# Addresses of stationary and moving operands in a hybrid decoder layer on one core

## Chip, cores and metric

One core of a Trainium2 chip runs the whole layer. The metric is the device time of one execution in microseconds (us); less is better. Spans, starts and durations of single instructions come from one profiled execution.

## The reference

`x` is 1 x 512 x 1024 in float32, and all products are wanted at float32 accuracy. Cut to what matters:

```python
h = rmsnorm(x, norm_mix_g)
q, k, v, xr, gr, g_attn, g_rnn = jnp.split(h @ w_in, offs, axis=-1)      # each 512 x 1024
attn_out = diff_attention(q, k, v, ...)        # 8 heads, two softmaxes a head, causal
rnn_out  = rg_lru_branch(xr, gr, ...)          # conv, gates, linear recurrence
merged = sigmoid(g_attn) * (attn_out @ w_pa) + sigmoid(g_rnn) * (rnn_out @ w_pr)
x = x + merged @ w_out
up = square(relu(rmsnorm(x) @ w_up))           # 512 x 4096
x = x + up @ w_down
```

## The kernel before

Every operand of a product is split into two float32r tiles, a high part and the rest, and a product is three matmuls: high x high, high x rest, rest x high (`mm3`, lines 124 to 127). The first operand named is the stationary one, loaded into TensorE 128 columns at a time; the second is the moving one, streamed past it with 256 or 512 columns. The stationary tile of the next matmul is loaded while the present one streams.

Weights come in units of 128 x 1024 (4 blocks of 128 rows, 256 columns). A load on SP's queue brings a unit into a raw buffer; ScalarE copies it to `whi`, VectorE writes the rest to `wlo` (`Weights.cast`, line 98; in the last stages `cast_hi` and `cast_lo`, lines 914 to 942). Four pairs of slots in pool `wp` hold cast units, and in the last stages every fifth unit (`own`, line 920) uses a pair in pool `fin` instead. A unit takes part in 24 matmuls. TensorE's instructions run in the order in which the program emits them; the other engines have an order of their own, kept by hand (`InOrder`).

The stages in order of time:

- The first gate blocks (lines 265 to 338): `hu` moving (512 columns), weights stationary. `two(k)` multiplies two blocks at once; the third block goes through `cols_proj` (line 137) with `hu` too. Then `hT`, the normalised input, is written over the pool `hp`.
- q, k, v (`qkv_pair`, `tok_proj`, line 220): here `hT` is stationary and the weights move, 256 columns. They fill the pauses of `attention` (line 492), whose logits multiply `qkT` tiles with each other, whose transposes have `pe` or `qn` stationary and `ident` moving (lines 459 and 541), and whose value product (`av`, line 547) has `v` stationary and `pt` moving, 256 columns.
- The remaining gates and the recurrent branch (`rnn_chunk`): `hT` moving, 512 columns. `y_attn` (line 742) multiplies `w_pa` with the attention's output `aT` between them.
- `y_rnn` (line 750) with `R` moving, then `merged` (line 834) with `mT` moving, all 512 columns.
- The MLP, from line 1054: three up pairs and then alternately down and up. An up step has `h2T` moving, 512 columns. A down step (line 1093, seven products in place of eight by sums of blocks) has `us` moving, 256 columns, in four stages of 336 matmuls (d = 0 to 3); stage d reads `forms[2d]` and `forms[2d + 1]`. `forms[n]` stands in `hp` if n % 3 is 0, else in `fin` as `us1` or `us2` (`up_out`, line 979).

In the built program the tiles begin, in bytes of a partition modulo 256, at: weight slots of `wp` 64; `hT`, `mT` and the `us` of `hp` 64; `hu`, `h2T`, `R`, `pt`, `v`, `pe`, `qn`, `ident`, the own slots and the `us` of `fin` 128; `qkT` and `aT` 224. All blocks within a tile lie a multiple of 512 bytes apart, so that the tiles' beginnings alone set the difference of two operands modulo 256.

GpSimd issues few DMAs: two small ones a head, and 16 in the down stages that add one raw block to another (lines 935 and 940). Their descriptors stand in a space at the beginning of each partition.

Of the kernel before, what the change touches and what calls it, by code (L numbers as in the profile page):

```python
# [11 lines left out]
F32 = mybir.dt.float32  # L12
F32R = mybir.dt.float32r
# [6 lines left out]
P = 128  # L20
# [3 lines left out]
KT = DM // P  # L24
# [13 lines left out]
def tile_block(ctx: ExitStack, tc: tile.TileContext, x, w_in, w_rga, w_rgx, w_pa, w_pr, w_o,  # L38
               w_up, w_dn, rel_bias, smalls, lamv, onehot, out):
    nc = tc.nc  # L40
# [3 lines left out]
    wp = ctx.enter_context(tc.tile_pool(name="wp", bufs=3))  # L44
# [33 lines left out]

    slots = [4]

    class Weights:
        def __init__(self, ahead, raws):
            self.reqs, self.raw, self.units = [], [], []
            self.pos, self.done, self.ahead, self.raws = 0, 0, ahead, raws

        def cols(self, w, c0, k0=0, n=KT):
            for k0 in range(k0, k0 + n, 4):
                self.reqs.append((w[k0 // 4, c0 // 256], 4))
            return self

        def fetch(self):
# [3 lines left out]
                nc.sync.dma_start(raw, src.rearrange("p (k c) -> p k c", k=a))  # L95
                self.raw.append(raw)

        def cast(self, pool=None):
            assert pool or slots[0] > 0
            slots[0] -= 0 if pool else 1  # L100
            self.fetch()
            n = len(self.units)
            raw, a = self.raw[n], self.reqs[n][1]
            hi, lo = ((pool or wp).tile([P, a, 1024 // a], F32R, tag=t, name=t, bufs=2 if pool else 4) for t in ("whi", "wlo"))
            A.copy(hi, raw)
            V.tensor_tensor(out=lo, in0=raw, in1=hi.bitcast(F32), op=ALU.subtract)
            self.raw[n] = None
            self.units.append((hi, lo))
            self.fetch()
# [121 lines left out]
    wa.cols(w_in, OGA + 512)  # L231
    for j in range(4):
        for o in (OQ, OK_, OV):
            wa.cols(w_in, o + 256 * j)
    wa.cols(w_in, OGA + 768)
    for j in range(4):
        wa.cols(w_in, OGR + 256 * j)
    for j in range(4):
        wa.cols(w_pa, 256 * j)
    wb = Weights(1, 1)  # L240
    for j in range(4):
        wb.cols(w_in, OX + 256 * j).cols(w_in, OG + 256 * j)
    for j in range(4):
        wb.cols(w_pr, 256 * j)
    for j in range(4):
        wb.cols(w_o, 256 * j)
    R, aT, mT = [None] * KT, [None] * NH, [None] * KT
# [17 lines left out]
    with tc.tile_pool(name="p1", bufs=1) as p1:  # L265
        on = p1.tile([P, P], F32, name="on")
        G.memset(on, 1.0)
        zero = p1.tile([P, 256], F32R, name="zero")
        V.memset(zero.bitcast(F32), 0.0)
        pw = psum("acc")  # L270
        for n in range(16):
            T.matmul(pw[:, :256], zero[:, :P], zero, start=True, stop=True)
        ssq = p1.tile([P, S], F32, name="ssq")
        xT = p1.tile([P, KT, S], F32, name="xT")
        hu = [p1.tile([P, KT, S], F32R, name=f"hu{z}", tag=f"hu{z}") for z in range(2)]
        raws = [[(wp if u else p1).tile([P, 4, 256], F32, name="wraw", tag="wraw", bufs=2) for u in range(2)] for z in range(2)]
        pieces = ((0, 1), (1, 2), (2, 4), (4, 6), (6, 8))
        for k0, k1 in pieces:
            nc.sync.dma_start(xT[:, k0:k1, :], x[k0 * P:k1 * P, :].rearrange("(k p) s -> p k s", p=P))
            if k0 == 0:  # L280
                nc.sync.dma_start(smt, smalls)
            for z in range(2):
                c0 = 256 * (k0 % 4)
                nc.sync.dma_start(raws[z][k0 // 4][:, k0 % 4:(k1 - 1) % 4 + 1, :],
                                  w_in[k0 // 4, OGA // 256 + z][:, c0:c0 + 256 * (k1 - k0)].rearrange("p (k c) -> p k c", c=256))
        wa.fetch()
        ws = [[[wp.tile([P, 4, 256], F32R, tag=t, name=t, bufs=4) for t in ("whi", "wlo")] for u in range(2)] for z in range(2)]
        ps = [[psum("at"), psum("at")] for z in range(2)]
        for k0, k1 in pieces:
            u, kk = k0 // 4, slice(k0 % 4, (k1 - 1) % 4 + 1)  # L290
            for k in range(k0, k1):
                split(hu[0][:, k, :], hu[1][:, k, :], xT[:, k, :], smt[:, C_G1 + k:C_G1 + k + 1])
                if k == k0:
                    for z in range(2):
                        split(ws[z][u][0][:, kk, :], ws[z][u][1][:, kk, :], raws[z][u][:, kk, :])
            for k in range(k0, k1):
                sq = ssq if k == 0 else p1.tile([P, S], F32, tag="sq", name="sq", bufs=2)
                A.activation(sq, xT[:, k, :], AF.Square)
                if k:
                    V.tensor_tensor(out=ssq, in0=ssq, in1=sq, op=ALU.add)  # L300

        def two(k):
            for z in range(2):
                for c in range(2):
                    w = ws[z][k // 4]
                    cs = slice(c * P, (c + 1) * P)
                    mm3(ps[z][c], (w[0][:, k % 4, cs], w[1][:, k % 4, cs]), (hu[0][:, k, :], hu[1][:, k, :]), k == 0, k == KT - 1)

        for k in range(6):
            two(k)  # L310
        slots[0] = 2
        wa.cast()
        pr = psum("at")
        for t in range(NT):
            T.matmul(pr[:, t:t + 1], ssq[:, t * P:(t + 1) * P], ones, start=True, stop=True)
        rs = sm.tile([P, NT], F32, tag="rs4", name="rs4")
        rstd_of(rs, pr[:, :NT], DM, NT)
        dg = p1.tile([P, S], F32, name="dg", tag="sq", bufs=2)
        for t in range(NT):
            A.activation(dg[:, t * P:(t + 1) * P], ident, AF.Copy, scale=rs[:, t:t + 1])  # L320
        two(6)
        wa.cast()
        rb = p1.tile([P, S], F32, name="rb")
        gu = cols_proj(wa, lambda k: (hu[0][:, k, :], hu[1][:, k, :]), lambda ps: gate_out(tga, 2, ps, rb))
        pb = psum("acc")
        T.matmul(pb, on, dg, start=True, stop=True)
        V.tensor_copy(rb, pb)
        two(7)
        slots[0] += 2
        for k in range(KT + 1):  # L330
            if k < KT:
                V.tensor_tensor(out=xT[:, k, :], in0=xT[:, k, :], in1=rb, op=ALU.mult)
            if k > 0:
                split(hT[0][:, k - 1, :], hT[1][:, k - 1, :], xT[:, k - 1, :], smt[:, C_G1 + k - 1:C_G1 + k])
                next(gu)
        wa.pump()
        for z in range(2):
            gate_out(tga, z, ps[z], rb)
# [19 lines left out]
    for half in range(2):  # L358
        PT.append([wk.tile([P, 2 + 2 * half, 256], F32R, name=f"pt{half}{z}", tag=f"pt{half}{z}") for z in range(2)])
        for z in range(2):  # L360
            G.memset(PT[half][z][:, 1 + 2 * half, 0:P].bitcast(F32), 0.0)

    def work(name):
        return wk.tile([P, S], F32, tag="pe", name=name, bufs=5)
# [549 lines left out]
    def cast_hi():  # L914
        n = len(units)
        plus(n)
        slots[0] -= 1
        kind, a, p = ops[n]
        src = raw[kind, a, p if kind == "up" else uses[p][0]]
        own = n % 5 == 4  # L920
        hi, lo = ((fin if own else wp).tile([P, 4, 256], F32R, tag=t, name=t, bufs=1 if own else 4) for t in ("whi", "wlo"))
        A.copy(hi, src)
        units.append((hi, lo))
        half.append((hi, lo, src, ops[n]))
# [54 lines left out]
    def up_out(a, ps):  # L979
        n = a // 2  # L980
        if a % 2 == 0:
            forms[n] = (hp if n % 3 == 0 else fin).tile([P, 2, 7, 2, 256], F32R, tag=("hT", "us1", "us2")[n % 3], name="us")
        d = forms[n][:, :, :, a % 2, :]
        q = fin.tile([P, 2, 2, 256], F32, tag="q", name="q")
        fs = fin.tile([P, 4, 256], F32, tag="fs", name="fs")
        w = 0.0 if a == 15 else 1.0
        for c in range(2):
            A.activation(q[:, c, ::-1, :], two(ps[c]), AF.Relu)
            A.activation(q[:, c], q[:, c], AF.Square)
        a11, a21, a22, a12 = q[:, 0, 1], q[:, 0, 0], q[:, 1, 0], q[:, 1, 1]  # L990

        def sums():
            for m, (x, y, op) in enumerate(((a21, a22, ALU.subtract), (fs[:, 0], a11, ALU.subtract), (a11, a21, ALU.subtract), (a12, fs[:, 1], ALU.add))):
                V.tensor_tensor(out=fs[:, m], in0=x, in1=y, op=op)

        def first_hi():
            hi_part(d[:, :, 0], a11)
            hi_part(d[:, :, 1:3], q[:, 1])

        def first_lo():  # L1000
            lo_part(d[:, :, 0], a11)
            lo_part(d[:, :, 1:3], q[:, 1])

        later(w * 1.0, first_hi)
        if w == 0:
            later(0.0, first_lo)
        later(w * 2.5, sums)
        later(w * 3.5, lambda: hi_part(d[:, :, 3:7], fs))
        if w:
            later(3.6, first_lo)  # L1010
        later(w * 5.0, lambda: lo_part(d[:, :, 3:7], fs))
# [129 lines left out]
```

## Time and profile before

| | |
|---|---|
| median of 3 runs | 881.33 us (881.31 to 881.35) |
| the profiled execution | 880.92 us |
| its span, first to last instruction | 879.2 us |
| TensorE: matmuls, busy | 5232, 871.2 us (99%) |
| TensorE: weight loads, busy | 5232, 762.6 us (87%) |
| VectorE, ScalarE, GpSimd busy | 602.2, 429.0, 64.4 us |
| DMA moved | 99.28 MB, 113 GB/s |

Matmuls overlap in the profile: the next one starts while the one before is still draining, so the mean length of one says little on how often one starts. Weight loads are a row of their own (PEld) and run beside the matmuls. In the table of windows a row gives the stretch, its length, the time TensorE was busy in it, in brackets the matmuls that lie in it or reach into it, the granted clock (1.00 is all of it), the DMA engines' busy share and GB/s.

### The profile page before, as it was taken

What the parts mean: (1) busy time and instruction counts of PE and PEld (TensorE: products, weight loads), DVE (VectorE), ACT (ScalarE), POOL (GpSimd) and SP (SyncE); (2) the same over time, 40 slices, a digit from 0 to 9 for tenths busy, and PEclk for the clock granted to TensorE, in tenths of its full rate; (3) what the DMA queues carried; (4) which work ended last, traced back from release to release, by engine and by line L of the source; (5) the groups of instructions that cost most, each with busy time, mean ns of one, the idle gap of its engine ahead of it and who ended that gap; (6) DMA issues with size and microseconds to landing.
All of it is one profiled execution on the core that took longest, in us unless ns stands there. A gap on an engine that the chain in (4) does not pass through costs nothing.

```text
span 879.2 us, 13193 instructions
## 1 busy us (share of the span) xinstructions
PE 871.2 (99%) x5232; PEld 762.6 (87%) x5232; DVE 602.2 (68%) x1040; ACT 429.0 (49%) x683; POOL 64.4 (7%) x72
## 2 busy tenths in 40 slices
PE   9999999999999999999999999999999999999997
PEld 7799999999888887888878888889988998899897
DVE  6765688887866346877876656767746775667586
ACT  7444355554555336577643235556335444544441
POOL 0030222113000000000000000000000000000000
PEclk9999999999999999999999999999999999999999
DMA  5347222131321342322213633223642364256353
GB/s 200 135 142 222 93 73 77 52 94 62 98 70 39 113 137 95 110 85 88 80 55 125 223 125 114 102 86 82 170 166 72 110 173 134 64 137 194 78 146 95
DMA packets 34238, 99.28 MB, mean 113 GB/s; under 512 B 3952, under 2 KB 8760, under 8 KB 34176
## 3 DMA queue, kind: packets, MB, share of 16 engines
q1 hardware_dynamic: 30976, 87.93, 30.3%
q0 software_dynamic: 3200, 10.50, 6.3%
q8 instruction: 41, 0.67, 0.3%
q14 instruction: 21, 0.17, 0.1%
HBM read 87.89 MB, written 4.76 MB: 105 GB/s over the span
## 4 chain that ended last, share of the span: by engine, by line
PE 88%; ACT 4%; DMA 3%; DVE 3%; issue 1%; SPq 0%; POOL 0%; ACTq 0%; DVEq 0%; POOLq 0%
PE acc L125 21%; PE acc L126 21%; PE acc L127 20%; PE acc L1093 17%; PE at L507 3%; DMA wraw<-in_w_in_dram 2%; ACT whi L66 1%; DVE wlo L66 1%; PE at L541 1%; PE at L126 1%; PE at L127 1%; PE at L125 1%; PE at L459 1%; PE at L572 1%; DMA xT<-in_x_dram 1%
## 5 line engine op out<-in xcount | busy, mean ns | idle before, releaser
L1093 PE MATMUL acc<-us,whi 128*128 128x256 f32 x896 | 158.9, 281 | 0.5 <-DVE x L66 0.5
L66 DVE TENSOR_TENSOR wlo<-wraw,whi 128x1024 fp32r<-128x1024 f32 (+2 forms) x86 | 96.9, 1148 | 67.9 <-ACT whi L66 67.6
L66 ACT CAST whi<-raw 128x1024 fp32r<-128x1024 f32 x88 | 90.5, 1048 | 104.2 <-DVE raw L66 39.4
L1093 PEld LDWEIGHTS acc<-us,whi 128*128 128x128 f32 x896 | 137.7, 189 | 1.2 <-DVE x L66 0.7
L1093 PE MATMUL acc<-us,wlo 128*128 128x256 f32 x448 | 125.4, 280 | 0.0
L66 DVE TENSOR_TENSOR wlo<-raw,whi 128x1024 fp32r<-128x1024 f32 x88 | 106.8, 1220 | 17.1 <-ACT whi L66 17.0
L125 PE MATMUL acc<-whi,hT 128*128 128x256 f32 x384 | 111.4, 290 | 0.0
L127 PE MATMUL acc<-whi,hT 128*128 128x256 f32 x384 | 108.9, 284 | 0.0
L126 PE MATMUL acc<-wlo,hT 128*128 128x256 f32 x384 | 108.9, 284 | 0.0
L66 ACT CAST whi<-wraw 128x1024 fp32r<-128x1024 f32 (+2 forms) x86 | 82.5, 982 | 50.0 <-DMA wraw<-in_w_in_dram 33.6
L126 PE MATMUL acc<-h2T,whi 128*128 128x512 f32 x256 | 100.5, 392 | 0.0
L125 PE MATMUL acc<-h2T,whi 128*128 128x512 f32 x256 | 100.1, 391 | 0.0
L127 PE MATMUL acc<-h2T,wlo 128*128 128x512 f32 x256 | 100.0, 390 | 0.0
L1093 PEld LDWEIGHTS acc<-us,wlo 128*128 128x128 f32 x448 | 84.2, 188 | 0.0
L125 PE MATMUL acc<-hT,whi 128*128 128x512 f32 x208 | 82.2, 395 | 0.0
L127 PE MATMUL acc<-hT,wlo 128*128 128x512 f32 x208 | 81.5, 392 | 0.0
L126 PE MATMUL acc<-hT,whi 128*128 128x512 f32 x208 | 81.5, 392 | 0.0
L125 PEld LDWEIGHTS acc<-whi,hT 128*128 128x128 f32 x384 | 73.2, 191 | 4.3 <-issue 3.0
L127 PEld LDWEIGHTS acc<-whi,hT 128*128 128x128 f32 x384 | 73.2, 191 | 0.8 <-issue 0.4
L126 PEld LDWEIGHTS acc<-wlo,hT 128*128 128x128 f32 x384 | 73.3, 191 | 0.7 <-issue 0.5
L66 ACT ACTIVATE pe<-pe,nm 128x128 f32<-128x128 f32 (+3 forms) x64 | 35.5, 556 | 65.4 <-DVE nm L66 65.4
L66 DVE TENSOR_TENSOR x<-acc,x 128x512 f32<-128x512 f32 x48 | 33.0, 688 | 40.9 <-PE acc L1093 31.5
(194 smaller groups left out, 1609.9 us busy)
## 6 DMA issues: line engine op xcount, KB each, us to landing
wraw<-in_w_in_dram SPq DMA_DIRECT2D x52, 512.0 KB, 3.5
raw<-in_w_up_dram SPq DMA_DIRECT2D x32, 512.0 KB, 4.4
raw<-in_w_dn_dram SPq DMA_DIRECT2D x32, 512.0 KB, 3.4
raw<-raw POOLq DMA_DIRECT2D x16, 512.0 KB, 4.5
wraw<-in_w_pa_dram SPq DMA_DIRECT2D x8, 512.0 KB, 4.3
wraw<-in_w_pr_dram SPq DMA_DIRECT2D x8, 512.0 KB, 3.4
wraw<-in_w_o_dram SPq DMA_DIRECT2D x8, 512.0 KB, 4.4
trep<-tdram SPq DMA_DIRECT2D x8, 320.0 KB, 4.9
```

Source lines behind the costliest of these rows:

```text
L66: ins = f(*a, **k)
L125: T.matmul(o, l[0], r[0], start=first, stop=False)
L126: T.matmul(o, l[0], r[1], start=False, stop=False)
L127: T.matmul(o, l[1], r[0], start=False, stop=last)
L459: T.transpose(out=ps[:, t * P:(t + 1) * P], in_=qn[t // 2][:, c0:c0 + P], identity=ident)
L507: T.matmul(lg[c][:, :N], qT[r, x0, i * P:(i + 1) * P], kT[r, y0, :N], start=a == 0, stop=a == 2)
L541: T.transpose(out=tp[:, b * P:(b + 1) * P], in_=st[s][:, b * P:(b + 1) * P], identity=ident)
L572: T.matmul(ps[:, t:t + 1], sq[:, t * P:(t + 1) * P], ones, start=True, stop=True)
L1093: T.matmul(b[:, 256 * u:256 * u + 256], l[:, i, P * u:P * u + P], act[:, r, f, i % 2], start=p in ("M1", "M2", "M5") and k == z == u == e ...
```

## The change

Only places in memory change; every instruction, its operands and its order stay.

- A slot for `whi` or `wlo` becomes 256 bytes longer, and a unit stands in it shifted by 0, 64 or 160 bytes (`weight_pair`). The shift is 64 for the first two gate blocks, for q, k, v, for `w_pr`, and for up and down in the shared slots; 160 for `w_pa`; 0 elsewhere, in the own slots too.
- The `us` tiles in `fin` become 256 bytes longer and are used from byte 192 on.
- A tile `apart` of 64 bytes stands ahead of `pe`, `qn`, `v` and the attention's output tiles.
- The space for descriptors of GpSimd's DMAs shrinks from 16384 (the default) to 8192 bytes of each partition, which makes the room.
- `cols` and `cast` lose parameters that nobody used.

By these sizes (8192, 4352 and 28928 bytes are multiples of 256) the difference of the moving operand's address and that of the stationary one, modulo 256, becomes:

| product (stationary, moving), columns | before | after |
|---|---|---|
| first two gate blocks (weights, `hu`), 512 | 64 | 0 |
| third gate block (weights, `hu`), 512 | 64 | 64 |
| q, k, v (`hT`, weights), 256 | 0 | 64 |
| value product (`v`, `pt`), 256 | 0 | 192 |
| transposes (`pe` or `qn`, `ident`), 128 | 0 | 192 |
| gates and recurrent inputs (weights, `hT`), 512 | 0 | 0 |
| `y_attn` (weights, `aT`), 512 | 160 | 0 |
| `y_rnn` (weights, `R`), 512 | 64 | 0 |
| output (weights, `mT`), 512 | 0 | 0 |
| up (weights, `h2T`), 512: shared, own slot | 64, 0 | 0, 0 |
| down (weights, `us` of `hp`), 256: shared, own slot | 0, 192 | 192, 192 |
| down (weights, `us` of `fin`), 256: shared, own slot | 64, 0 | 192, 192 |

```diff
+    def weight_pair(shift, own=None):
+        ts = [(own or wp).tile([P, 1024 + 64], F32R, tag=t, name=t, bufs=1 if own else 4) for t in ("whi", "wlo")]
+        return [t[:, shift // 4:shift // 4 + 1024].rearrange("p (k c) -> p k c", k=4) for t in ts]
...
-        def cols(self, w, c0, k0=0, n=KT):
-            for k0 in range(k0, k0 + n, 4):
+        def cols(self, w, c0, shift=0):
+            for k0 in range(0, KT, 4):
                 self.reqs.append((w[k0 // 4, c0 // 256], 4))
+                self.shift.append(shift)
...
-            hi, lo = ((pool or wp).tile([P, a, 1024 // a], F32R, tag=t, name=t, bufs=2 if pool else 4) for t in ("whi", "wlo"))
+            hi, lo = weight_pair(self.shift[n])
...
         for o in (OQ, OK_, OV):
-            wa.cols(w_in, o + 256 * j)
+            wa.cols(w_in, o + 256 * j, 64)
...
-        wa.cols(w_pa, 256 * j)
+        wa.cols(w_pa, 256 * j, 160)
...
-        wb.cols(w_pr, 256 * j)
+        wb.cols(w_pr, 256 * j, 64)
...
-        ws = [[[wp.tile([P, 4, 256], F32R, tag=t, name=t, bufs=4) for t in ("whi", "wlo")] for u in range(2)] for z in range(2)]
+        ws = [[weight_pair(64) for u in range(2)] for z in range(2)]
...
+    wk.tile([P, 16], F32, name="apart")
...
         own = n % 5 == 4
-        hi, lo = ((fin if own else wp).tile([P, 4, 256], F32R, tag=t, name=t, bufs=1 if own else 4) for t in ("whi", "wlo"))
+        hi, lo = weight_pair(0 if own else 64, fin if own else None)
...
-            forms[n] = (hp if n % 3 == 0 else fin).tile([P, 2, 7, 2, 256], F32R, tag=("hT", "us1", "us2")[n % 3], name="us")
+            t = hp.tile([P, 7168], F32R, tag="hT", name="us") if n % 3 == 0 else fin.tile([P, 7168 + 64], F32R, tag=f"us{n % 3}", name="us")
+            t = t if n % 3 == 0 else t[:, 48:48 + 7168]
+            forms[n] = t.rearrange("p (r f h s) -> p r f h s", r=2, f=7, h=2)
...
-    nc = _bacc.Bacc("TRN2", target_bir_lowering=False, num_devices=1)
+    nc = _bacc.Bacc("TRN2", target_bir_lowering=False, num_devices=1, dynamic_dma_scratch_size=8192)
```

## Rows read from the trace of the kernel before

**Rows 1.** The page's head: the span, and busy time, share and instructions of each engine.
```profile
span 879.2 us, 13193 instructions
PE 871.2 (99%) x5232; PEld 762.6 (87%) x5232; DVE 602.2 (68%) x1040; ACT 429.0 (49%) x683; POOL 64.4 (7%) x72
```

**Rows 2.** The list of waits of TensorE's matmuls, the first and the last of six: total us, times, longest.
```profile
PE acc L272 <- DVE zero L66: 1.2, 1, 1.2
...
PE at L125 <- ACT tt L66: 0.2, 1, 0.2
```

**Rows 3.** Windows of TensorE over stretches of 512 columns, in this order: `hT` (83 matmuls), `mT` (192), `h2T` with an own slot (24), `R` (120), `h2T` with shared slots (96), `aT` (20).
```profile
292.15:310.97 18.82, 18.82 (x85) 1.00 0.39 112
495.02:538.59 43.57, 43.57 (x194) 1.00 0.45 156
588.41:593.85 5.44, 5.44 (x25) 1.00 0.38 72
462.06:489.52 27.46, 27.46 (x121) 1.00 0.39 125
566.44:588.41 21.97, 21.97 (x97) 1.00 0.29 96
446.24:450.92 4.68, 4.68 (x21) 1.00 0.28 103
```

**Rows 4.** Windows of TensorE over stretches of 256 columns, in this order: q, k, v (95 matmuls); the first down stage (336) and in it an own-slot unit (24); the second, the third and the fourth down stage (336 each); then inside the third stage its first units in shared slots (71), an own-slot unit (24), four shared-slot units (96), and, after the next own-slot unit, four more (96).
```profile
45.07:56.45 11.38, 11.38 (x96) 1.00 0.34 107
605.07:644.95 39.88, 39.88 (x338) 1.00 0.59 167
610.79:613.59 2.80, 2.80 (x27) 1.00 0.12 22
...
688.88:728.73 39.85, 39.85 (x337) 1.00 0.57 164
772.70:811.57 38.87, 38.87 (x338) 1.00 0.60 169
833.54:874.40 40.86, 40.39 (x337) 1.00 0.44 122
772.70:781.06 8.36, 8.36 (x72) 1.00 0.39 99
781.06:783.93 2.87, 2.87 (x27) 1.00 0.57 184
783.93:794.81 10.88, 10.88 (x98) 1.00 0.53 143
797.69:808.57 10.88, 10.88 (x98) 1.00 0.94 273
```

**Rows 5.** Groups of TensorE's matmuls by line and shape (the forms kept apart): count, busy us, mean ns of one, idle before. Lines 125, 126 and 127 have the same counts, so one of the three is shown.
```profile
L1093 PE MATMUL acc<-us,whi 128*128 128x256 f32 x896 | 158.9, 281 | 0.5 <-DVE x L66 0.5
...
L125 PE MATMUL acc<-whi,hT 128*128 128x256 f32 x384 | 111.4, 290 | 0.0
...
L125 PE MATMUL acc<-h2T,whi 128*128 128x512 f32 x256 | 100.1, 391 | 0.0
...
L125 PE MATMUL acc<-aT,whi 128*128 128x512 f32 x64 | 25.3, 396 | 0.0
L125 PE MATMUL acc<-R,whi 128*128 128x512 f32 x64 | 25.3, 395 | 0.7 <-ACT whi L66 0.7
...
L541 PE MATMUL at<-ident,pe 128*128 128x128 f32 x80 | 14.3, 276 | 0.0
L125 PE MATMUL at<-pt,v 128*128 128x256 f32 x48 | 14.0, 292 | 0.0
...
L459 PE MATMUL at<-ident,qn 128*128 128x128 f32 x64 | 9.9, 274 | 0.0
```

**Rows 6.** The chain that ended last, in order of time (start us, us, what): where it comes to TensorE after the beginning, and the first piece and the return to TensorE of its two later stretches through other engines.
```profile
28.85 1.10 PE acc L326 x2
...
294.85 0.60 ACT gate L66
...
342.10 0.50 PE at L125
...
439.91 0.69 ACT tt L66
...
456.33 0.50 PE acc L125
```

**Rows 7.** Windows of the matmuls of one tile alone: the first two rows are of `aT`, the third of `R`.
```profile
295.00:345.00 50.00, 9.40 (x36) 1.00 0.39 121
...
442.00:456.00 14.00, 8.49 (x35) 1.00 0.12 39
...
442.00:456.00 14.00, 5.99 (x24) 1.00 0.12 39
```

**Rows 8.** The instructions that write or read the raw blocks of the last stages (count: shortest/median/longest ns, first and last start) and the idle time of an engine until such a DMA (us, times); then the page's row of these DMAs (count, KB each, median us from issue to landing).
```profile
L66 DVE TENSOR_TENSOR wlo<-raw,whi x88: 1162/1220/1228, 532.9 to 865.7; 128x1024 fp32r<-128x1024 f32 x88
...
L66 POOL DMA_DIRECT2D raw<-raw x16: 850/859/902, 590.6 to 860.0; - x16
...
  DMA raw<-raw: 20.0, 4
...
raw<-raw POOLq DMA_DIRECT2D x16, 512.0 KB, 4.5
```

More of the change, by code (lines that the diff above doesn't have):

```diff
@@ L79, in tile_block @@
     slots = [4]
+    def weight_pair(shift, own=None):
+        ts = [(own or wp).tile([P, 1024 + 64], F32R, tag=t, name=t, bufs=1 if own else 4) for t in ("whi", "wlo")]
+        return [t[:, shift // 4:shift // 4 + 1024].rearrange("p (k c) -> p k c", k=4) for t in ts]
     class Weights:
         def __init__(self, ahead, raws):
-            self.reqs, self.raw, self.units = [], [], []
+            self.reqs, self.raw, self.units, self.shift = [], [], [], []
             self.pos, self.done, self.ahead, self.raws = 0, 0, ahead, raws
-        def cols(self, w, c0, k0=0, n=KT):
-            for k0 in range(k0, k0 + n, 4):
+        def cols(self, w, c0, shift=0):
+            for k0 in range(0, KT, 4):
                 self.reqs.append((w[k0 // 4, c0 // 256], 4))
+                self.shift.append(shift)
             return self
@@ L96, in fetch, with cast @@
                 self.raw.append(raw)
-        def cast(self, pool=None):
-            assert pool or slots[0] > 0
-            slots[0] -= 0 if pool else 1
+        def cast(self):
+            assert slots[0] > 0
+            slots[0] -= 1
             self.fetch()
```

## The prediction

> **What bounds the kernel now.** I read the page's head first: TensorE is busy 871.2 of 879.2 us [rows 1], and its granted clock is 1.00 in every window read below [rows 3, 4]. The list of waits comes next: TensorE's idle time with a named releaser is six waits, 3.3 us in all, from 1.2 us down to 0.2 us [rows 2]. So almost the whole span is the sum of the distances from one matmul's start to the next, and "busy" hides how large these are: a matmul of 512 columns is shown as 390 ns long, though one starts every 227 to 234 ns. I therefore read distances, by windows that begin and end on starts of matmuls of one kind. A window's time divided by its matmuls gives the distance; its count also holds the one or two that still drain as it opens, so a unit of 24 reads x25 to x27.
>
> Sorted by what the diff touches, the difference of addresses (moving tile minus the stationary tile that is loaded meanwhile, modulo 256 bytes), the windows separate.
>
> At 512 columns [rows 3]: difference 0 gives 18.82/83 = 226.7 ns (hT), 43.57/192 = 226.9 (mT) and 5.44/24 = 226.7 (h2T against the own weight slot). Difference 64 gives 27.46/120 = 228.8 (R) and 21.97/96 = 228.9 (h2T against a shared slot). Difference 160 gives 4.68/20 = 234.0 (aT). The two h2T windows touch, run one line on one operand, and differ in the slot alone; so the slot's address is the cause that is left.
>
> At 256 columns [rows 4]: difference 0 gives 11.38/95 = 119.8 (q, k, v) and 2.87/24 = 119.6 (a down unit from the own slot). Difference 64 has two steady values: 8.36/71 = 117.7 in the first three units of the third down stage, and 10.88/96 = 113.3 in the four units after each of its first two own-slot units. Difference 192 never runs alone: an own-slot unit in the first down stage has it in half of its matmuls and 0 in the other half, 2.80/24 = 116.7; with 119.6 for the zero half, 113.8 is left for the other.
>
> **The change part by part.** The counts are from the groups of instructions by form [rows 5]. No instruction is added or removed and no order changes; every queue keeps its sequence, so no new instruction waits in front of others.
>
> 1. Up, 768 matmuls (3 x 256): 27 of the 32 units use shared slots, 27 x 24 = 648, and go from 64 to 0: 648 x (228.9 - 226.7) = 1.4 us.
> 2. The recurrent projection (R), 192 matmuls, 64 to 0. The chain of waits has TensorE in it only from 456.33 on [rows 6], and the first unit of 24 runs before that [rows 7], so 168 remain: 168 x 2.1 = 0.4 us.
> 3. The attention projection (aT), 192 matmuls, 160 to 0: 192 x 7.2 = 1.4 us. But from 294.85 to 342.10 and from 439.91 to 456.33 the chain runs through weight loads, casts and the recurrence, not through TensorE [rows 6], and 36 + 35 of these matmuls lie about there [rows 7]. What they save becomes waiting for ScalarE, VectorE and loads. The other 121 give 0.9 us.
> 4. The first gates (hu), 8 x 2 x 2 x 3 = 96 matmuls by lines 303 to 307, 64 to 0: 0.2 us, of which I take 0.1, since the chain enters TensorE for good only at 28.85 [rows 6]. The third gate block keeps 64.
> 5. q, k, v: 3 x 384 = 1152 matmuls, 0 to 64. All lie on TensorE's path. They gain 2.1 ns each (2.4 us) if they settle at 117.7, and 6.5 ns (7.5 us) if at 113.3. I take 117.7: these stretches of 24 to 96 start behind other work (transposes, logits), as the 117.7 window does, while both 113.3 windows start behind a unit at difference 0. The lower end is no gain.
> 6. Down: 4 stages of 336, now at mixed differences, go to 192 throughout. They take 39.88, 39.85, 38.87 and 40.86 us [rows 4]. 336 x 113.4 = 38.1 us, so the first three gain 1.8, 1.75 and 0.8; the last holds pauses (0.5 us idle in its own row), and I give it 1.8 as well: 6.1 us. That a long run at 192 holds 113.4 is inferred from half units only. The other end is 117.7, the slow value at 64: 39.5 us a stage, no gain in sum.
> 7. Attention's value product, 144 matmuls (3 x 48) of 0 to 192, in runs of 6 and 12: 3 ns each, 0.4 us; the ends are 0 and 0.9.
> 8. The transposes (80 + 64) get the padded tile as stationary operand, 0 to 192. No row shows 128 columns at another difference. With the widest swing seen at 256 columns, 6.4 ns, the bound is 0.9 us either way; between equal ends I take 0.
> 9. Casts, copies and loads cost nothing more: the raw buffers don't move, and the subtraction that writes a weight's low part takes 1162 to 1228 ns over all 88, into shared and own slots alike [rows 8], though these start at 64 and 128. Their cover is the casting ahead; if it went, TensorE would show waits for whi or wlo. It holds at the new pace: no wait stands in the windows that already run at 113.3 [rows 4].
> 10. The descriptor space of the DMAs that GpSimd issues is halved: no cost taken; its price is the last rival's.
>
> The sum: 1.4 + 0.4 + 0.9 + 0.1 + 2.4 + 6.1 + 0.4 = 11.7 us. The profiled execution took 880.92 us (span 879.2 and 1.7 around it), which gives 869.2. The median of the runs shown is 881.33, 0.4 above that execution, so the forecast is 869.6.
>
> One rule speaks against all of it. The rows show that the slot's address alone moves the distance, by 2.2 ns in two windows that touch [rows 3]. The Trainium skill, "TensorE: Matmul & The Clock Gate", section "Step-by-step: what each phase is for", says that TensorE reads SBUF through two independent ports and that "Loading the next tile's weights doesn't steal SBUF read bandwidth from the running matmul." By that rule placement would change nothing and the time would stay at 881.3. The trace does not agree, by those 2.2 ns and by the 6.3 ns between the two down windows.
>
> **The rivals.**
> - Both fast: q, k, v settle at 113.3 as well. For it: eight of the eleven shared-slot units of the third down stage run there. Against: the only long run at 64 that follows other work stayed slow for 71 matmuls. 869.6 - 5.1 = 864.5.
> - Down slow: at 192 the long runs settle near 117.7 instead of 113.4. For it: 64 has two steady values, so 192 may. Against: the half units, which reach 113.8 although they are interrupted every six matmuls. 869.6 + 6.1 = 875.7.
> - Swallowed: TensorE's gain before 295 us (q, k, v and value product, 2.8 us) becomes waiting, because VectorE's softmax steps or casts are next. For it: the chain does leave TensorE later [rows 6]. Against: no named wait of the whole run is longer than 1.2 us [rows 2], and the chain stays on TensorE from 28.85 on until then. 872.4.
> - Nothing: the distances depend on something that goes with the slots, such as the time at which their units run, and not on addresses. Against: in the first down stage own-slot units are faster than the stage's mean (116.7 against 118.7), in the third slower (119.6 against 115.7) [rows 4]; a slot that is fast or slow by itself can't do both. 881.3.
> - Slower: the halved descriptor space. Place: the 16 additions of one raw block to another that GpSimd issues in the down stages; each lands 4.5 us after its issue [rows 8]. If half the space made one wait for its own first half, it would land another 4.5 us later. The casting ahead covers most, but four times an engine sat idle until such an addition landed, 20.0 us in all [rows 8]; there nothing covers it: 4 x 4.5 = 18 us, 887.6. It decides from 11.7/4 = 2.9 us more on each. Against: the issue takes a steady 850 to 902 ns, which shows no wait for space.
>
> **How the numbers follow.** Forecast 0.45, both fast 0.19, down slow 0.14, swallowed 0.09, nothing 0.07, slower 0.06. The likeliest is 869.6. Its own range, with parts 3, 4, 7 and 8 at either end, is 867.5 to 871.5. The range that should hold 8 in 10 reaches from both fast to down slow: 864.0 to 876.0; outside lie "nothing", "slower", and the tails. A measurement of this kernel can tell about 0.2% (1.8 us) from no change. The first four cases are faster by more than that, and some tails of "nothing" too: faster 0.88, same 0.06, slower 0.06.
>
> **What the profile of the changed kernel would show.** Up units from shared and own slots alike at 226.7 ns, aT at 227 instead of 234, R at 227; hT in its 512-column stretches unchanged. A down stage of 336 in 38.1 us (39.5 for the slow case). q, k, v at 117.7 in the windows that now read 119.8; 113.3 would be the fast rival, 119.8 would kill part 5. In the two stretches of rows 6 the aT gain should show as longer waits. GpSimd's additions should still land in 4.5 us. I am wrong in the main step if the down stages don't fall to one common time, or if any 256-column stretch gets slower at its new difference.

## The result

| | before | after |
|---|---|---|
| median | 881.34 us (881.31 to 883.08) | 876.74 us (875.32 to 877.57, 4 runs) |
| profiled execution | 880.92 us | 877.57 us |

The ratio is 0.9942 [0.993, 0.9955]: 4.6 us faster, where 11.7 were forecast. The direction was right; the time lies 0.7 us above the upper end of the range, next to the rival "down slow" (875.7). The profiled execution is the slowest of the changed kernel's four.

The page's head of the changed kernel, beside [rows 1]: TensorE is still the bound, with the same instructions and 5.1 us less time shown as busy.

```profile
span 875.8 us, 13193 instructions
PE 866.1 (99%) x5232; PEld 758.7 (87%) x5232; DVE 601.9 (69%) x1040; ACT 428.9 (49%) x683; POOL 64.4 (7%) x72
```

The windows of TensorE in the changed kernel; they hold the same matmuls as [rows 3, 4]. First 512 columns: `hT` (83 matmuls), `mT` (192), `h2T` with an own slot (24), `R` (120), `h2T` with shared slots (96), `aT` (20).

```profile
289.98:308.87 18.89, 18.89 (x85) 1.00 0.37 112
493.88:537.41 43.53, 43.53 (x194) 1.00 0.45 158
586.90:592.34 5.44, 5.44 (x25) 1.00 0.38 72
461.24:488.44 27.20, 27.20 (x122) 1.00 0.41 129
565.14:586.90 21.76, 21.76 (x97) 1.00 0.29 97
445.32:449.92 4.60, 4.60 (x22) 1.00 0.27 105
...
45.11:56.30 11.19, 11.19 (x97) 1.00 0.34 110
67.28:75.21 7.93, 7.93 (x72) 1.00 0.67 213
603.45:643.02 39.57, 39.57 (x337) 1.00 0.60 170
686.54:726.12 39.58, 39.58 (x338) 1.00 0.58 167
769.64:809.21 39.57, 39.57 (x338) 1.00 0.59 166
830.97:870.87 39.90, 39.30 (x337) 1.00 0.44 122
857.82:870.87 13.05, 13.05 (x117) 1.00 0.34 83
```

Read them as before, time by matmuls. `h2T` against shared slots is now at 21.76/96 = 226.7 ns, as against its own slot, and `R` is too. `aT` went from 234.0 to 230.0 ns, not to 226.7. The lines behind the dots are 256 columns: a q, k, v stretch at 11.19/95 = 117.8 and one at 7.93/70 = 113.3, under one difference. Then come the four down stages and the end of the fourth. The first three hold 39.57/336 = 117.8 ns throughout. The third has thereby lost what it had: it took 38.87 us before. Only parts of the fourth ran at 113 to 114, as its end at 13.05/115 = 113.5.

TensorE's waits (us in all, times, longest), beside [rows 2]:

```profile
PE at L130 <- ACT tt L66: 1.4, 1, 1.4
PE acc L277 <- DVE zero L66: 1.2, 1, 1.2
PE acc L130 <- ACT whi L66: 0.8, 1, 0.8
```

The first of these was 0.2 us long before. It stands in front of the first recurrent gates, where the timeline shows TensorE idle for 1.42 us:

```profile
341.36 0.50 PE L130 MATMUL at<-xh,gw 128*128 128x512 f32 x1 [1.42 <-ACT tt L66]
```

GpSimd's additions of raw blocks, beside [rows 8], are as before: the issue takes the same time, the landing 4.6 us instead of 4.5.

```profile
L66 POOL DMA_DIRECT2D raw<-raw x16: 850/859/902, 589.1 to 857.2; - x16
...
raw<-raw POOLq DMA_DIRECT2D x16, 512.0 KB, 4.6
```

Since TensorE runs the same matmuls in the same order in both traces, the distances can be added up by the operand of the matmul that ends each. In us of the profiled executions (3.36 in all, where the medians differ by 4.6):

```
distance ends at          forecast    gained
q, k, v                        2.4      2.91
up (h2T)                       1.4      1.58
down (us)                      6.1      0.68
value product                  0.4      0.31
y_attn (aT)                    0.9      0.28
y_rnn (R)                      0.4      0.12
first gates (hu)               0.1     -0.11
other gates (hT)               0       -0.19
transposes                     0       -0.63
first recurrent gates (xh)     0       -1.29
all others                     0       -0.30
```

Down is the term that failed. About 1.3 us was given back at one wait, and 0.55 of the transposes' loss is two pauses too (109 to 394 ns and 230 to 500 ns between two starts).

### The profile page after: what moved, and what is told of

Read it like the earlier page. It is cut to its first block, busy times and chain, and to the rows that moved or that the text cites. A ratio compares the mean times of both kernels' runs of the same rounds, so it can differ in the third digit from the quotient of the medians.

```text
span 875.8 us, 13193 instructions
## 1 busy us (share of the span) xinstructions
PE 866.1 (99%) x5232; PEld 758.7 (87%) x5232; DVE 601.9 (69%) x1040; ACT 428.9 (49%) x683; POOL 64.4 (7%) x72
## 4 chain that ended last, share of the span: by engine, by line
PE 85%; DVE 5%; ACT 4%; DMA 4%; issue 1%; SPq 0%; POOL 0%; ACTq 0%; POOLq 0%; DVEq 0%
PE acc L130 20%; PE acc L132 20%; PE acc L131 20%; PE acc L1102 17%; DMA wraw<-in_w_in_dram 3%; PE at L514 2%; DVE wlo L66 2%; ACT whi L66 2%; PE at L131 1%; PE at L548 1%; PE at L130 1%; PE at L132 1%; PE at L466 1%; PE at L579 1%; DVE x L66 1%
## 5 line engine op out<-in xcount | busy, mean ns | idle before, releaser
L130 PE MATMUL acc<-whi,hT 128*128 128x256 f32 x384 | 110.1, 287 | 0.0
L132 PE MATMUL acc<-whi,hT 128*128 128x256 f32 x384 | 107.5, 280 | 0.0
L130 PEld LDWEIGHTS acc<-whi,hT 128*128 128x128 f32 x384 | 72.1, 188 | 4.3 <-issue 3.0
L132 PEld LDWEIGHTS acc<-whi,hT 128*128 128x128 f32 x384 | 72.1, 188 | 0.7 <-issue 0.4
```

Of the source, the lines that this page charges most:

```text
L130: T.matmul(o, l[0], r[0], start=first, stop=False)
L132: T.matmul(o, l[1], r[0], start=False, stop=last)
```

## The experiments

Theory: the difference of the two addresses modulo 256 sets the distance; at 64 and 192 the 256-column work has two steady distances, 113.3 and 117.8 ns, and what a stretch gets is decided where it starts. Rivals: the distance goes with slots, sizes or times rather than addresses; each difference has one distance of its own; the wait at the recurrent gates swallows whatever is gained before it. Edits are against the changed kernel.

**The same kernel again**, for what varies by itself.

> The changed kernel once more, for a second profile. Theory (two steady distances at 256 columns, 113.3 and 117.8 ns, and what runs just before a stretch picks one): the first three down stages read 39.6 us (117.8 ns) again, since they are entered the same way, from 512-column matmuls; in q, k, v most stretches read 117.8 and a few 113.3, and which ones are fast may differ from the first profile, by its timing. Rival (the difference of addresses alone sets the distance): every stretch has the same value in both profiles. Time by both 875.3 to 877.6 us.

876.17 us, ratio 0.9937 [0.9922, 0.9951]. The first three down stages repeat to 0.01 us. Of the 26 stretches of q, k, v with 20 matmuls or more, 2 ran at 113.3, both where the first trace has it too; a third of that trace ran at 117.8 here. The distance between the two starts at the first recurrent gates, 1819 ns in the first trace, was 1158. The third gate block (`hu`, difference 64 in every kernel) took 229.1 ns a matmul here and 233.3 in the first trace.

**All the layout, none of the differences.** Sizes and descriptor space as changed, but every operand where the old differences come out.

```diff
     def weight_pair(shift, own=None):
+        shift = 0
...
-    wk.tile([P, 16], F32, name="apart")
...
-            t = t if n % 3 == 0 else t[:, 48:48 + 7168]
+            t = t if n % 3 == 0 else t[:, 0:7168]
```

> The changed kernel with every shift at 0 and without the 64-byte tile: slots and tiles stay 256 bytes longer and the descriptor space stays at 8192 bytes, so that the differences modulo 256 are those of the kernel before while everything else of the change stays. Theory (only the differences modulo 256 count): 881.3 us within 0.5, q, k, v at 119.8 ns, up at 228.9, the down stages at 39.9, 39.9, 38.9 and 40.9 us. Rival (part of the 4.6 us gain comes from other places, or the halved descriptor space costs something that hid more gain): 879 or less, or 883 or more.

881.54 us, ratio 1.0001 [0.9992, 1.0011]. The distances of before are back: windows of the first and the third down stage, of q, k, v (95 matmuls) and of `h2T` with shared slots (96), beside [rows 3, 4].

```profile
604.88:644.76 39.88, 39.88 (x338) 1.00 0.59 167
772.51:811.38 38.87, 38.87 (x338) 1.00 0.59 169
44.16:55.55 11.39, 11.39 (x97) 1.00 0.34 107
566.25:588.22 21.97, 21.97 (x97) 1.00 0.29 96
```

So the shifts are the whole effect, and the halved descriptor space costs nothing. This settles the rivals "nothing" and "slower". That the difference counts, and not one operand's address alone, the rows of before show: with the weights at 64 `hT` and `mT` took 226.7 to 226.9 ns, `R` and `h2T` 228.8 to 228.9, and `h2T` took 226.7 with the weights at 128 [rows 3].

**q, k, v back at difference 0.**

```diff
-            wa.cols(w_in, o + 256 * j, 64)
+            wa.cols(w_in, o + 256 * j)
```

> The changed kernel with q, k, v weights back at shift 0 (difference 0), the rest as changed. Theory: their 1152 matmuls go back to 119.8 ns and the gain of 2.5 us between the first and the last of them is lost: 879.2 us. Rival (that gain is swallowed before the end by the recurrent branch, where 1.2 us were lost again): only 1.3 us or less is lost, 878 us.

878.47 us, ratio 0.9967 [0.9954, 0.998]: 2.3 us worse than the changed kernel on the same chip, with 11.39/95 = 119.9 ns again. Part 5 is worth what it was said to be, and the time keeps it, against the rival of this run.

**Up and down as before.**

```diff
-        hi, lo = weight_pair(0 if own else 64, fin if own else None)
+        hi, lo = weight_pair(0, fin if own else None)
...
-            t = t if n % 3 == 0 else t[:, 48:48 + 7168]
+            t = t if n % 3 == 0 else t[:, 0:7168]
```

> The changed kernel with the up and down stages back at the differences of before (weights at shift 0, the us tiles at their beginning), the rest as changed. Prediction's terms (1.4 for up, 6.1 for down): 7.5 us slower, 883.7 us. Theory (down at 192 stays in the slow state of 117.8 ns, 39.6 us a stage; up as predicted): 1.4 + 0.9 = 2.3 us slower, 878.5 us.

878.82 us (877.06 to 879.64, 9 runs), ratio 0.9965 [0.9955, 0.9975]: 2.1 to 2.7 us worse than the two medians of the changed kernel, where parts 1 and 6 together were forecast at 7.5. The third stage is back at 38.87 us, the first two at 39.88 and 39.86.

**`w_pa` back at difference 160.**

```diff
-        wa.cols(w_pa, 256 * j, 160)
+        wa.cols(w_pa, 256 * j)
```

> The changed kernel with the attention projection's weights back at shift 0 (difference 160), the rest as changed. Prediction's term (121 of the 192 matmuls on the path, 7.2 ns each): 0.9 us slower, 877.1 us. Theory after the first profiles (aT runs in groups of three to six between other products, takes 230.3 ns there even at difference 0 and disturbs hT behind it, so that the stage gained 0.1 us): 0.2 us or less, 876.3 us, aT at 234 ns.

877.16 us, ratio 0.9955 [0.994, 0.997], 0.4 to 1.0 worse than the changed kernel, whose own runs spread over 2 us. The profiled run shows two pauses at 311 and 312 us, 988 and 923 ns between two starts. The first stands in no other trace; at the second place several other kernels paused too (up to 806 ns), the changed kernel for 405 ns at most. So the time alone doesn't settle part 3. Over all its matmuls (distances under 300 ns) `aT` took 232.7 ns here, 231.1 in the changed kernel and 232.6 before: the gain is 1.5 ns, not 7.2.

**A down stage that starts at difference 0**, as the units did that ran at 113.3 before.

```diff
-        hi, lo = weight_pair(0 if own else 64, fin if own else None)
+        at0 = kind == "dn" and a[1] == 0 and p == "M1"
+        hi, lo = weight_pair((192 if own else 0) if at0 else (0 if own else 64), fin if own else None)
```

> The changed kernel with one unit of 24 matmuls in each of the four down stages, the first, at difference 0 instead of 192. Theory (two steady distances; leaving a unit at difference 0 leads into the fast one): that unit reads 119.5 to 120 ns, the 13 others 113.3 instead of 117.8, so a stage takes 2.87 + 13 x 2.72 = 38.2 us instead of 39.6 in the first three, 4 us less in all: 872.5 us. Rival (117.8 ns is what difference 192 gives): the unit costs 0.05 us more a stage and the others stay at 117.8: 876.9 us.

876.09 us, ratio 0.9936 [0.9919, 0.9952]. The expectation failed. The windows of its first stage: the whole, the unit at 0, the 13 units at 192 behind it.

```profile
602.11:641.72 39.61, 39.61 (x337) 1.00 0.59 170
602.11:604.98 2.87, 2.87 (x26) 1.00 0.73 137
604.98:641.72 36.74, 36.74 (x314) 1.00 0.58 172
```

The unit at 0 takes 119.6 ns, and 36.74/312 = 117.8 follows: starting from 0 alone does not choose the short distance at 192.

**Other differences, first look.** Each q, k, v request has a difference of its own. The down stages, whose shifts are set unit by unit in `cast_hi` (not shown), have 32, 96, 128 in the first, 160, 224, 16 in the second, one unit at 0 and 13 at 64 in the third, and 64 throughout in the fourth.

```diff
-            wa.cols(w_in, o + 256 * j, 64)
+            wa.cols(w_in, o + 256 * j, (16, 32, 48, 96, 112, 128, 144, 160, 176, 192, 208, 224)[3 * j + o // DM])
...
```

> A look at other differences; only slots' shifts differ from the changed kernel. The twelve requests of q, k, v stand at differences 16, 32, 48, 96, 112, 128, 144, 160, 176, 192, 208, 224 in turn; the down stages have, unit by unit, 32 x5, 96 x5, 128 x4 (first), 160 x5, 224 x5, 16 x4 (second), one unit at 0 and 13 at 64 (third), 64 throughout (fourth). Theory (two steady states, 113.3 and 117.8, for differences that are not near 0): every one of the others shows one of these two values. Rival (the distance is a function of the difference): the values spread, and one difference gives 113.3 in all of its stretches. Third stage: 113.3 behind the unit at 0 if what mattered in the kernel before was the step from 0 to 64; 117.8 if it was something else.

878.43 us, one run. Windows of stretches of q, k, v at 96 (46 matmuls), 112 (46) and 192 (43), then of down at 32 (119), 96 (120) and 128 (96), then of the third stage (0, then 64), its 13 units at 64, and the first 71 of the fourth, at 64 throughout.

```profile
80.80:86.31 5.51, 5.51 (x47) 1.00 0.82 235
101.03:106.29 5.26, 5.26 (x48) 1.00 0.30 100
181.82:186.71 4.89, 4.89 (x45) 1.00 0.20 48
...
604.34:618.23 13.89, 13.89 (x121) 1.00 0.53 152
618.23:632.62 14.39, 14.39 (x122) 1.00 0.55 126
632.62:644.01 11.39, 11.39 (x99) 1.00 0.71 245
...
771.14:809.37 38.23, 38.23 (x337) 1.00 0.60 171
773.89:809.37 35.48, 35.48 (x315) 1.00 0.61 177
831.15:839.52 8.37, 8.37 (x73) 1.00 0.25 74
```

Differences do have distances of their own: 119.8 at 96, 114.3 at 112, 113.7 at 192, and in the down stages 116.7 at 32, 119.9 at 96, 118.6 at 128. (The second stage had 118.7 at 160, 118.3 at 224, 119.9 at 16.) So the expectation that every other difference shows 113.3 or 117.8 failed, and its rival holds in part. But 64 still shows both values in one trace: 35.48/313 = 113.4 behind the unit at 0, and 8.37/71 = 117.9 without it. The third stage, at 38.23 us, is what part 6 had forecast (38.1).

**Other differences, second look.** q, k, v at 192. First stage: two units at 64, one at 0 (it is an own-slot unit), 11 at 64; second: 64 throughout; third: two at 192, one at 0 (in a shared slot), 11 at 64; fourth: 192. The edits are of the same kind as in the first look.

> Only slots' shifts differ from the changed kernel. q, k, v stand at difference 192 instead of 64; the down stages, unit by unit, at 64, 64, 0, then 64 x11 (first), 64 x14 (second), 192, 192, 0, then 64 x11 (third), 192 x14 (fourth, as changed). Theory (two states; 64 behind a unit at 0 is fast): first and third stage 117.8, 117.8, 119.6, then 113.3, 38.5 us each; the second, entered from 512 columns, 117.8 throughout, 39.6 us. Rival (only the own slot behind three units at 64 did it): the first stage stays at 117.8 behind its unit at 0. q, k, v at 192: 117.8 with some stretches at 113.3, as at 64.

874.56 us, one run. The first and the third stage, the last 263 matmuls of the third, and the second stage:

```profile
601.25:640.87 39.62, 39.62 (x337) 1.00 0.58 170
767.57:806.02 38.45, 38.45 (x338) 1.00 0.61 170
...
776.17:806.02 29.85, 29.85 (x266) 1.00 0.66 190
684.44:724.02 39.58, 39.58 (x338) 1.00 0.58 166
```

The expectation for the first stage failed: 64 behind an own-slot unit at 0 stayed at 117.8, although in the third stage of before it went to 113.3 behind one. In the third stage here it went to 29.85/263 = 113.5, behind a unit at 0 in a shared slot. q, k, v at 192 had a mean of 115.2 ns, against 117.1 at 64.

**Both gains together.** q, k, v at 192, and in the next kernel at 112; the first three down stages one unit at 0, then 13 at 64; the fourth at 192.

```diff
-            wa.cols(w_in, o + 256 * j, 64)
+            wa.cols(w_in, o + 256 * j, 192)
...
-        hi, lo = weight_pair(0 if own else 64, fin if own else None)
+        if kind == "up":
+            s = 0 if own else 64
+        else:
+            d, u = a[0], sum(o[0] == "dn" and o[1][0] == a[0] for o in ops[:n])
+            s = (-(((0,) + (64,) * 13 if d < 3 else (192,) * 14)[u]) - (64 if own else 0)) % 256
+        hi, lo = weight_pair(s, fin if own else None)
```

> The changed kernel with q, k, v at difference 192 instead of 64, and the first three down stages at 0 for their first unit and at 64 for the 13 others. Theory (two states; the step from 0 to 64 led into the fast one in one stage of an earlier run, and 192 in q, k, v was fast in 60% of its matmuls): down stages of 2.88 + 13 x 2.72 = 38.2 us instead of 39.6, 4 us in all, and 2 us in q, k, v; 870.2 us. Rival (which state a stretch falls into depends on the phase at its entry and not on the step of differences): one or more of the three stages stays at 39.6 us, 871.5 to 874.

> As both_192, with q, k, v at difference 112, which in the sweep gave 113.3 ns in most of the one request that had it. Theory (two states, with shares of the fast one that go with the difference): if 112 keeps its 114.3 ns over all twelve requests, 1 us less than both_192, 869.2 us; if the sweep's request was lucky, the same as both_192 or up to 2 us more.

870.31 us, ratio 0.9885 [0.987, 0.9899], and 870.03, ratio 0.9879 [0.9864, 0.9894]. In both, the three stages take 38.23 us each. At 192, 16 of the 26 q, k, v stretches ran at 113.5 to 114.3 and the rest at 117.6 to 117.8 (mean of all distances 115.6). At 112 none of 40 matmuls or more stayed at 117.8: they ran at 113.8 to 114.6, as in this kernel's windows of 95, 70 and 46 matmuls, and their last ten distances at 113.3 to 113.5 (mean of all 114.9). So both forecasts (870.2 and 869.2) came true within 0.9 us.

```profile
44.72:55.53 10.81, 10.81 (x97) 1.00 0.35 109
66.30:74.27 7.97, 7.97 (x72) 1.00 0.68 212
78.91:84.17 5.26, 5.26 (x48) 1.00 0.68 227
```

At the first recurrent gates there were 295 ns between the two starts at 192 and 600 at 112, against 555 in the trace of before and 1819 in the changed kernel's; yet TensorE came there with a lead of 4.1 and 4.3 us on before, twice the changed kernel's 2.0. The wait does not swallow a lead as such.

**What that wait is.** The chain of the changed kernel in front of it (start us, us, what), from the point where it leaves TensorE; then the same load in the chain of before, and the chain's beginning and end at 112:

```profile
292.68 0.60 ACT gate L66
...
327.72 1.05 ACT whi L66
...
328.80 1.24 DVE wlo L66
...
330.05 5.76 DMA wraw<-in_w_in_dram
...
335.89 1.06 ACT whi L66
...
336.97 1.23 DVE wlo L66
338.20 1.28 DVE q L66 x3
...
339.50 0.62 ACT q L66
...
332.29 4.25 DMA wraw<-in_w_in_dram
...
290.45 0.60 ACT gate L66
...
337.87 0.49 PE at L130
```

In this stretch the chain goes from cast to load to cast: a load of a weight unit starts when the casts have emptied a raw buffer, and VectorE reaches the recurrence's work behind these casts. From `gate` to the recurrent gates it took 47.25 us before [rows 6], 48.68 in the changed kernel and 47.42 at 112. TensorE's lead is handed on, since the chain begins earlier by as much; what the changed kernel lost lies in the chain's length, and nearly all of it in the one load that took 5.76 us instead of 4.25. So a third raw buffer should remove the wait:

```diff
-                raw = wp.tile([P, a, 1024 // a], F32, tag="wraw", name="wraw", bufs=2)
+                raw = wp.tile([P, a, 1024 // a], F32, tag="wraw", name="wraw", bufs=3)
...
-    wb = Weights(1, 1)
+    wb = Weights(1, 2)
...
```

The other tiles that share these buffers get three as well. With it TensorE's matmuls also stand in another order at 28 places.

> The changed kernel with three raw buffers in the shared pool instead of two and two loads ahead instead of one for the second weight stream; the first raw block of a stream then waits for no cast of the other. Theory (from 293 to 342 us load, cast and load again form a ring that sets the end, and swallows 0.5 to 1.3 us of TensorE's lead): the waits at the first recurrent gates (1.2 to 1.8 us in the changed kernel's profiles) fall to 0.6 or less, and 0.5 to 1.5 us are gained, 875.2 us. Rival (that wait is for the recurrence's own work on VectorE and ScalarE): the wait stays, 876.3 us.

874.11 us, ratio 0.9925 [0.9909, 0.9942]. The wait is gone (261 ns), and the one before `R` fell from 1235 to 819 ns between its starts. The third of its waits, 0.8 in the changed kernel:

```profile
PE acc L130 <- ACT whi L66: 0.4, 1, 0.4
```

That is 2.1 to 2.6 us below the changed kernel's two medians, where 0.5 to 1.5 were expected. Beside the second profile of the changed kernel, 2.8 us are gained: 1.3 at these two waits, 0.8 in q, k, v, where more stretches ran at 113.3, and about 1 in the first 31 us, where a wait of 0.4 us for ScalarE's `dg` is gone too. What removed that one was not tested.

**The same with both gains** (112).

> both_112 and third_raw together: q, k, v at difference 112, the first three down stages at 0 for one unit and then at 64, and three raw buffers. Theory (the two edits act in different stages; third_raw was 2.1 us below the changed kernel, of which some 0.6 is the luck of its q, k, v stretches): 1.5 us below both_112's 870.0, 868.5 us, with the down stages at 38.2 us again. Rival (in both_112 no long wait stood at the first recurrent gates, so there is nothing left for the third buffer to take away but the 0.4 us at the recurrent projection): 869.6 us.

868.3 us (867.91 to 868.97), ratio 0.9855 [0.9837, 0.9872]: the best version, and 0.2 us from its forecast. Its profiled execution is 1.4 us shorter than that of the kernel at 112 with two buffers, 0.7 of it at the two waits. Its three stages, and the fourth, which stayed at 39.9 us:

```profile
598.45:636.68 38.23, 38.23 (x337) 1.00 0.63 175
680.22:718.45 38.23, 38.23 (x337) 1.00 0.60 167
761.99:800.22 38.23, 38.23 (x338) 1.00 0.62 169
821.99:861.90 39.91, 39.31 (x337) 1.00 0.40 109
```

## Why the prediction was wrong, point by point

- **The step that failed is part 6**, where it says that a long run at 192 holds 113.4, "inferred from half units only". It held 117.8 in every unit at 192 of the first three stages, in every kernel that had it there, and down gained 0.68 us of the 6.1. The half units of the trace of before did come down to 113 to 114 within six matmuls; what failed was to carry a distance from runs of six matmuls, entered from 0 or 64, to a run of 336. The value 113.8 was itself read too low: start by start, the sixes at 192 in that own-slot unit take 115.5 ns on average and those at 0 take 117.7, not 119.6. The same trace held a warning: sixes at 64 in the shared slots of that stage settled at 117 to 119, though long runs at 64 in the third stage reached 113.3. By the forecast's own numbers this costs 3 x 336 x 4.4 ns = 4.4 us in the first three stages (5.4 with the fourth, where some units behind pauses reached 113.3). The third alone became 0.7 us slower than before, since its units in shared slots had largely been at 113.3 already [rows 4]; that is the text's own sign of being wrong, a 256-column stretch that gets slower. The forecast had the other case as the rival "down slow" and gave it 0.14. That rival's reason, two steady distances at 64, was the right one; part 5 used it for q, k, v and part 6 did not.
- **Part 5** was right: 117.8 in most stretches, 113.3 in a few. 2.91 us instead of 2.4. "Both fast" did not come about at 64.
- **Part 1** was right: 226.7 ns, 1.58 us instead of 1.4.
- **Part 3** mis-sized a term. 7.2 ns came from a window of twenty [rows 3], but 19 of its 28 runs are sixes between stretches of `hT`, too short for the distance to settle: 1.5 ns on average. In the run of twenty it comes to 226 to 227 from the tenth matmul on. Of its stretch before the recurrence the text had rightly said that nothing would be gained.
- **Part 2** had the right distance, but of its 0.4 us the wait in front of `R` took back 0.17 (1063 to 1235 ns between two starts).
- **Parts 7, 8, 10**: 0.31 of 0.4 us; the transposes lost 0.63, inside the bound of 0.9 and mostly by two pauses; the descriptor space cost nothing, shown by the kernel without differences.
- **Swallowed**, a rival with 0.09, came true in part: some 2.4 us of pauses grew (1.26 at the recurrent gates, the rest in five pieces of 0.17 to 0.29), but not as told there. It was not TensorE's lead that was eaten, since kernels with twice the lead kept it, but one ring of load, cast and load, whose loads vary from execution to execution (the one above took 4.25 to 5.76 us). Had that wait not grown, the changed kernel's profiled execution would have come to about 876.3 at best, so this alone does not explain the miss.

**What stays open**: what chooses between 113.3 and 117.8 where a stretch starts. Of the runs with one unit at 0 first in the stage, 64 behind it was short in 10 of 10 stages and 192 in 0 of 3. 64 throughout was long in both stages that had it. Behind three units at 64 and one at 0, 64 was short in the trace of before and in the kernels that repeat it; behind two at 64 and one at 0 it was long in the one stage tried, and behind two at 192 and one at 0 short in the one stage tried. Pauses tell the two apart as well: in the fourth stage some units behind them came to 113.3 at 192 in all ten traces that have it there, and none at 64 in the one trace. In q, k, v the choice changes between two executions of one kernel at 64, and at 192 between two kernels that are alike in that part. Why the difference sets the distance at all is open too. No run here separates the addresses of the stretch before from the exact time of its last matmul.

The Trainium skill, "TensorE: Matmul & The Clock Gate", section "Step-by-step: what each phase is for", has the next weights load through a port of its own that takes nothing from the running matmul. The measurements decide against it as a rule that placement changes nothing: the kernel that undoes the differences alone is 5.4 us slower than the one with them on the same chip. Whether the weight load takes reads from the matmul, or something else holds it up, no run here shows.

## What to carry to other kernels

Where weights are reloaded for every matmul, divide windows of TensorE by their matmuls and sort the distances by the difference of the two operands' addresses modulo 256; busy shares show none of it. A distance seen in short, interrupted runs is no price for a long one: take it from a run of the length, the difference and the start that the new kernel will have, and where the trace shows two values for one difference, give both a full chance. When the engine that bounds the kernel gets faster by about one per cent, look for rings of load and cast that were just in time: here one load that varied by 1.5 us took back a quarter of the gain.

## What the runs showed of the hardware

- At 256 columns the distance depends on the difference modulo 256: about 119.8 ns at 0 and 96, 116.7 at 32 (down stage), 113.3 or 117.8 at 64 and 192, 113.5 to 114.6 at 112 (stretches of 40 and more, no other value in the two kernels at 112). At 512 columns it is 226.7 at 0, 228.9 at 64 and 234.0 at 160.
- Two steady distances stand at one and the same difference (64 or 192), and a run at it without pauses kept the one that it started with, for as long as 336 matmuls. At 512 columns the third gate block at difference 64 has two as well, about 229 and 233.3 ns in different executions.
- After a change of operand, some matmuls pass before the new distance is reached: at 512 columns and difference 0, `aT`, mostly in runs of six, took 230.3 ns in the median of its threes (the three matmuls of one product), where long stretches take 226.7.
